# Lp pooling on one core: the first load goes out as two halves of 64 rows, on two queues

## The chip, the core and the metric

The kernel runs on one core of a Trainium2 chip. The metric is the device time of one launch in microseconds, the median of several runs; lower is better. The core's engines take part as follows: ScalarE (ACT) squares and takes roots, VectorE (DVE) adds, SyncE (SP) and ScalarE issue the transfers between HBM and SBUF, and 16 DMA engines carry them out. TensorE and GpSimd compute nothing here.

## The reference

```python
x: float32 [32, 256, 4096]; p = 2.0; kernel_size = 4
out_length = length // kernel_size            # 1024
for i in range(out_length):
    window = np.abs(x[:, :, 4 * i:4 * i + 4]) ** p
    result[:, :, i] = np.mean(window, axis=-1) ** (1.0 / p)
```

With p = 2 this is, for every four neighbours, the square root of the mean of their squares. 134.2 MB are read and 33.6 MB are written.

## The kernel before

The input is taken as one flat array, since windows of four never cross a channel. It is cut into six blocks (`blocks`, line 51), each block into 128 rows, one for each SBUF partition, and the rows of a block into tiles along their length. There are 20 tiles; most are 128 x 13184 floats (`W`, 52,736 bytes in each partition, 6592 KB in all), the last is 128 x 11680. Three tiles fit at a time: tile i lies in `x_tiles[i % 3]`, printed `xt` in the profile.

Each tile goes through the same steps:

- `load(i)` (line 79, its DMA on line 83) brings the tile in with one DMA on SP's queue.
- `square` (line 89, ACT) squares it in place.
- `pairs` (line 95, DVE) adds elements 0 and 2, and 1 and 3, of each window, into the first half of the same tile.
- `fours` (line 99, DVE) adds the two sums of each window into the output tile `ot`, into the PSUM tile `st` or into a free part of an `xt`.
- `root` (line 102, ACT) takes the square root of a quarter of the sum, for one to three tiles at a time.
- `store(b, queue)` (line 86) writes a block of four tiles back with one DMA: blocks 0 to 2 are issued on the ACT queue, blocks 3 to 5 on SP.

The order of instructions on each engine is written out by hand (`manual_schedule`), and the framework adds the semaphore waits that the data need. Where one wait already follows from another, `implied(later, earlier)` (line 118) takes it away:

```python
    def implied(later, earlier):

        tc.declare_no_dep(later.ins, earlier.ins, reason="implied by the other waits")

    for i in range(X_SLOTS):
        load(i)
```

Loads 0, 1 and 2 are issued at once, ahead of everything else. In the loop over tiles 0 to 16 (line 130), load i + 3 stands behind the two sums of tile i: SP waits for them, as the slot is free only then. ACT's first instructions are the load of its function table and a root of one column (`first`), and then the square of tile 0, which waits for load 0.

Block 4 is stored by `store(4, nc.sync)` and block 5, the last tile alone, by `store(5, nc.sync)`, which is the last transfer of the program.

Of the kernel before, what the change touches and what calls it, by code (L numbers as in the profile page):

```python
# [1 line left out]

# [4 lines left out]


@with_exitstack
def kernel(  # L10
    ctx: ExitStack,
    tc: tile.TileContext,
    x: bass.AP,
    p: float,
    kernel_size: int,
    out: bass.AP,
):

    nc = tc.nc

    assert float(p) == 2.0, "kernel specialized for p == 2"
    k = int(kernel_size)  # L30
    assert k == 4, "kernel specialized for kernel_size == 4"

    P = nc.NUM_PARTITIONS
    fp32 = mybir.dt.float32
    Act = mybir.ActivationFunctionType
    add = mybir.AluOpType.add
    xf = x.rearrange("b c l -> (b c l)")
    of = out.rearrange("b c l -> (b c l)")
    total = xf.shape[0] // P

    W = 13184
    R = W // k
    X_SLOTS = 3
    NARROW = W - 32
    LAST = total - 18 * W - NARROW
    widths = [W] * 3 + [NARROW] + [W] * 15 + [LAST]
    n = len(widths)
    assert 0 < LAST <= W and LAST % 16 == 0


    blocks = [[0, 1, 2, 3], [4, 5, 6, 7], [8, 9, 10, 11], [12, 13, 14, 15], [18, 16, 17], [19]]
    block_of = {i: b for b, group in enumerate(blocks) for i in group}
    block_width = [sum(widths[i] for i in group) for group in blocks]

    x_pool = ctx.enter_context(tc.tile_pool(name="x_pool", bufs=1))
    o_pool = ctx.enter_context(tc.tile_pool(name="o_pool", bufs=1))
    s_pool = ctx.enter_context(tc.tile_pool(name="s_pool", bufs=1, space=bass.MemoryType.PSUM))
    x_tiles = [x_pool.tile([P, W], fp32, name=f"xt{j}") for j in range(X_SLOTS)]
    o_tile = o_pool.tile([P, 4 * R], fp32, name="ot")
    first = o_pool.tile([P, 1], fp32, name="first")  # L60
    s_tile = s_pool.tile([P, 4096], fp32, name="st")
    ctx.enter_context(tc.manual_schedule())

    def rows(flat, b, div):
        at = sum(block_width[:b]) * P // div
        return flat[at:at + block_width[b] * P // div].rearrange("(p w) -> p w", p=P)


    free = x_tiles[17 % X_SLOTS]
    place = {i: o_tile[:, i % 4 * R:i % 4 * R + widths[i] // k] for i in range(16)}  # L70
    place[18] = free[:, R:2 * R]
    place[19] = free[:, 0:LAST // k]
    place[16] = free[:, 2 * R:3 * R]
    place[17] = free[:, 3 * R:4 * R]
    held = [o_tile[:, 0:w // k] for w in block_width[:4]] + [free[:, R:4 * R], place[19]]

    xs, loads, stores, sums, squares = {}, {}, {}, {}, {}

    def load(i):
        b = block_of[i]  # L80
        at = sum(widths[j] for j in blocks[b][:blocks[b].index(i)])
        xs[i] = x_tiles[i % X_SLOTS][:, 0:widths[i]]
        loads[i] = nc.sync.dma_start(out=xs[i], in_=rows(xf, b, 1)[:, at:at + widths[i]])  # L83

    def store(b, queue):
        stores[b] = queue.dma_start(out=rows(of, b, k), in_=held[b])  # L86

    def square(v):
        return nc.scalar.activation(out=v, in_=v, func=Act.Square)  # L89

    def pairs(v):

        q = v.rearrange("p (n j) -> p n j", j=k)
        h = v[:, 0:v.shape[1] // 2].rearrange("p (n j) -> p n j", j=2)
        return nc.vector.tensor_tensor(out=h, in0=q[:, :, 0:2], in1=q[:, :, 2:4], op=add)  # L95

    def fours(o, v):
        h = v[:, 0:v.shape[1] // 2].rearrange("p (n j) -> p n j", j=2)
        return nc.vector.tensor_tensor(out=o, in0=h[:, :, 0], in1=h[:, :, 1], op=add)  # L99

    def root(o, s):
        return nc.scalar.activation(out=o, in_=s, func=Act.Sqrt, scale=1.0 / k)  # L102

    summed = {i: s_tile[:, 0:R] if i in (4, 8, 12, 16) else place[i] for i in range(n)}

    def roots(*group):
        if len(group) == 1:
            root(place[group[0]], summed[group[0]])
        else:
            v = o_tile[:, group[0] % 4 * R:(group[-1] % 4 + 1) * R]  # L110
            r = root(v, v)
            if group[0] in (5, 9):

                implied(r, stores[block_of[group[0]] - 1])
        if group[-1] in (3, 7, 11):
            store(block_of[group[-1]], nc.scalar)
# [9 lines that stand above are left out]
    ahead = {4: (3,), 8: (7,), 12: (11,)}  # L126
    behind = {3: [(0, 1, 2)], 7: [(5, 6), (4,)], 11: [(9, 10), (8,)], 14: [(12,)], 15: [(13, 14)], 16: [(15,)]}

    root(first[:, :], nc.const_aps.tensor(1.0, (P, 1), fp32))
    for i in range(17):  # L130
        if i in ahead:
            roots(*ahead[i])
        s = square(xs[i])
        squares[i] = s
        if i == 3:
            implied(s, squares[0])
        if i in (3, 7, 11):

            for earlier in sums[i - X_SLOTS]:
                implied(s, earlier)  # L140
        for group in behind.get(i, []):
            roots(*group)
        sums[i] = pairs(xs[i]), fours(summed[i], xs[i])
        if i + X_SLOTS < n:
            load(i + X_SLOTS)

    store(3, nc.sync)
    square(xs[17])
    pairs(xs[17])
    fours(summed[17], xs[17])  # L150
    later = {18: 4608, 19: 2000}

    def shared_square(i):
        v = xs[i][:, 0:later[i]]
        nc.vector.tensor_tensor(out=v, in0=v, in1=v, op=mybir.AluOpType.mult)  # L155
        square(xs[i][:, later[i]:widths[i]])

    def shared_pairs(i):
        implied(pairs(xs[i]), loads[i])

    shared_square(18)
    roots(16)
    roots(17)
    shared_pairs(18)
    fours(summed[18], xs[18])
    shared_square(19)
    roots(18)
    store(4, nc.sync)
    shared_pairs(19)
    fours(summed[19], xs[19])  # L170
    roots(19)
    store(5, nc.sync)


# [1 line left out]
_INS = ['x', 'p', 'kernel_size']  # L176
_OUTS = [((32, 256, 1024), 'float32')]

_NUMBERS = {'p': 2.0, 'kernel_size': 4}


# [26 lines left out]
```

## Time and profile before

| What | us |
|---|---|
| Median of 3 runs (394.01 to 394.08) | 394.02 |
| The profiled execution's own time | 394.04 |
| Span of its profile | 392.3 |
| ACT busy | 274.4 (70%) |
| DVE busy | 218.2 (56%) |
| Packets of the SP queue (q1), share of 16 DMA engines | 87.4% |
| Packets of the ACT queue (q10), share of 16 DMA engines | 11.9% |
| Mean rate over the span | 428 GB/s |

The profiled execution's time stands 1.7 us above its span; that part lies outside the recorded instructions. Times in the views count from the start of the span. The DMA queue lines give packets, megabytes and the time that the packets took, as a share of what 16 DMA engines could have worked in the span. In the chain of waits, each piece is what held up the next one, followed back from the last instruction. In the windows view, the DMA share is 1.00 where all 16 engines are busy; a packet's bytes count at its start, so that in short windows the rate swings and only its place in time is to be read.

### The profile page before, as it was taken

What the parts mean: (1) busy time and instruction counts of PE and PEld (TensorE: products, weight loads), DVE (VectorE), ACT (ScalarE), POOL (GpSimd) and SP (SyncE); (2) the same over time, 40 slices, a digit from 0 to 9 for tenths busy, and PEclk for the clock granted to TensorE, in tenths of its full rate; (3) what the DMA queues carried; (4) which work ended last, traced back from release to release, by engine and by line L of the source; (5) the groups of instructions that cost most, each with busy time, mean ns of one, the idle gap of its engine ahead of it and who ended that gap; (6) DMA issues with size and microseconds to landing.
All of it is one profiled execution on the core that took longest, in us unless ns stands there. A gap on an engine that the chain in (4) does not pass through costs nothing.

```text
span 392.3 us, 176 instructions
## 1 busy us (share of the span) xinstructions
DVE 218.2 (56%) x42; ACT 274.4 (70%) x37; POOL 0.2 (0%) x4
## 2 busy tenths in 40 slices
DVE  0009477580693274905942748069418485699970
ACT  1095695979950859799509597995098999969910
POOL 0000000000000000000000000000000000000000
DMA  8999999999999999999999999999999999999997
GB/s 344 430 430 430 430 440 435 452 457 366 430 430 430 430 430 430 430 441 446 452 446 441 436 430 436 430 430 430 430 430 430 430 430 430 430 453 415 430 413 342
DMA packets 3744, 167.77 MB, mean 428 GB/s; under 512 B 416, under 2 KB 416, under 8 KB 416
## 3 DMA queue, kind: packets, MB, share of 16 engines
q1 hardware_dynamic: 3312, 147.53, 87.4%
q10 hardware_dynamic: 432, 20.25, 11.9%
HBM read 134.22 MB, written 33.55 MB: 428 GB/s over the span
## 4 chain that ended last, share of the span: by engine, by line
DMA 43%; ACT 30%; DVE 23%; issue 0%; ACTq 0%; SPq 0%; DVEq 0%
DMA xt<-in_x_dram 43%; ACT xt L89 28%; DVE xt L95 14%; DVE ot L99 5%; DVE xt L99 3%; DVE xt L155 2%; ACT ot L102 2%; ACT xt L102 1%; ACTq L86 0%; SPq L83 0%; DVEq L95 0%
## 5 line engine op out<-in xcount | busy, mean ns | idle before, releaser
L89 ACT ACTIVATE xt<-xt 128x13184 f32<-128x13184 f32 (+3 forms) x20 | 216.7, 10847 | 92.3 <-DMA xt<-in_x_dram 91.0
L95 DVE TENSOR_TENSOR xt<-xt 128x6592 f32<-128x6592 f32 (+2 forms) x20 | 139.7, 6985 | 144.1 <-ACT xt L89 143.9
L99 DVE TENSOR_TENSOR ot<-xt 128x3296 f32<-128x3296 f32 (+1 forms) x13 | 46.7, 3592 | 17.9 <-DMA out_dram<-ot 17.6
L102 ACT ACTIVATE ot<-ot 128x6592 f32<-128x6592 f32 (+3 forms) x8 | 37.2, 4655 | 7.0 <-DVE ot L99 7.0
L102 ACT ACTIVATE xt<-xt 128x3296 f32<-128x3296 f32 (+1 forms) x3 | 8.5, 2836 | 8.8 <-DVE xt L99 8.8
L99 DVE TENSOR_TENSOR st<-xt 128x3296 f32<-128x3296 f32 x4 | 14.4, 3600 | 0.1
L99 DVE TENSOR_TENSOR xt<-xt 128x3296 f32<-128x3296 f32 (+1 forms) x3 | 10.4, 3461 | 0.1
L102 ACT ACTIVATE ot<-st 128x3296 f32<-128x3296 f32 x3 | 8.7, 2898 | 0.0
L155 DVE TENSOR_TENSOR xt<-xt 128x4608 f32<-128x4608 f32 (+1 forms) x2 | 7.2, 3593 | 0.0
L102 ACT ACTIVATE xt<-st 128x3296 f32<-128x3296 f32 x1 | 2.9, 2898 | 0.0
L102 ACT ACT_TABLE_LOAD x1 | 1.3, 1283 | 0.7 <-PEq L189 0.7
L102 ACT ACTIVATE first<-const-float32-1.0 128x1 f32<-128x1 f32 x1 | 0.2, 202 | 0.0
L189 POOL MEMSET const-bfloat16-1.0<- 128x1 bf16 x1 | 0.1, 101 | 0.0
L189 POOL MEMSET const-uint8-127<- 128x1 uint8 x1 | 0.1, 101 | 0.0
L189 POOL MEMSET const-float32-0.0<- 128x1 f32 x1 | 0.1, 98 | 0.2 <-issue 0.2
L189 POOL MEMSET const-float32-1.0<- 128x1 f32 x1 | 0.1, 98 | 0.0
## 6 DMA issues: line engine op xcount, KB each, us to landing
xt<-in_x_dram SPq DMA_DIRECT2D x18, 6592.0 KB, 29.8
out_dram<-ot ACTq DMA_DIRECT2D x2, 6592.0 KB, 35.1
out_dram<-ot SPq DMA_DIRECT2D x1, 6592.0 KB, 37.1
out_dram<-ot ACTq DMA_DIRECT2D x1, 6588.0 KB, 36.3
xt<-in_x_dram SPq DMA_DIRECT2D x1, 6576.0 KB, 24.7
xt<-in_x_dram SPq DMA_DIRECT2D x1, 5840.0 KB, 21.9
out_dram<-xt SPq DMA_DIRECT2D x1, 4944.0 KB, 16.1
out_dram<-xt SPq DMA_DIRECT2D x1, 1460.0 KB, 8.2
```

Source lines behind the costliest of these rows:

```text
L89: return nc.scalar.activation(out=v, in_=v, func=Act.Square)
L95: return nc.vector.tensor_tensor(out=h, in0=q[:, :, 0:2], in1=q[:, :, 2:4], op=add)
L99: return nc.vector.tensor_tensor(out=o, in0=h[:, :, 0], in1=h[:, :, 1], op=add)
L102: return nc.scalar.activation(out=o, in_=s, func=Act.Sqrt, scale=1.0 / k)
L155: nc.vector.tensor_tensor(out=v, in0=v, in1=v, op=mybir.AluOpType.mult)
L189: nc = _bacc.Bacc("TRN2", target_bir_lowering=False, num_devices=1)
```

## The change

Load 0 becomes two DMAs of 64 rows each. Rows 64 to 127 go out on the ScalarE queue, as ACT's first instruction, ahead of its table load; rows 0 to 63 go out on SP, in load 0's old place. All other loads stay as they were. Since load 0 is now two transfers, load 3 (the next one into the same slot) and the two sums of tile 0 would wait for both; these waits are declared away, because the sums wait for the square, which waits for both halves, and load 3 waits for the sums.

```diff
+    halves = []
 
     def load(i):
         b = block_of[i]
         at = sum(widths[j] for j in blocks[b][:blocks[b].index(i)])
         xs[i] = x_tiles[i % X_SLOTS][:, 0:widths[i]]
-        loads[i] = nc.sync.dma_start(out=xs[i], in_=rows(xf, b, 1)[:, at:at + widths[i]])
+        v = rows(xf, b, 1)[:, at:at + widths[i]]
+        if i == 0:
+            halves.append(nc.scalar.dma_start(out=xs[i][P // 2:P, :], in_=v[P // 2:P, :]))
+            halves.append(nc.sync.dma_start(out=xs[i][0:P // 2, :], in_=v[0:P // 2, :]))
+        else:
+            loads[i] = nc.sync.dma_start(out=xs[i], in_=v)
+            if i == X_SLOTS:
+                for half in halves:
+                    implied(loads[i], half)
...
         sums[i] = pairs(xs[i]), fours(summed[i], xs[i])
+        if i == 0:
+            for half in halves:
+                for s in sums[i]:
+                    implied(s, half)
         if i + X_SLOTS < n:
             load(i + X_SLOTS)
```

## The prediction, on record before the changed kernel ran

> **What bounds the kernel now.** I read the page's DMA queues first, then the chain of waits, then the windows, and last the first five microseconds.
>
> From the page:
>
> ```profile
> span 392.3 us, 176 instructions
> ...
> DMA  8999999999999999999999999999999999999997
> ...
> q1 hardware_dynamic: 3312, 147.53, 87.4%
> q10 hardware_dynamic: 432, 20.25, 11.9%
> ```
>
> The two queues' packets fill 87.4 + 11.9 = 99.3% of what 16 DMA engines can do in the span, 389.5 of 392.3 us. Only the first and the last slice are not full. The kernel is bound by its transfers from the first row to the last, and there is no idle DMA time in the middle into which a late start could vanish. ACT (70%) and DVE (56%) have room.
>
> The chain of waits and the timeline (start, duration, what; in the timeline, what ended the idle time before it):
>
> ```profile
> 0.73 18.04 DMA xt<-in_x_dram
> ...
> 18.79 11.20 ACT xt L89
> ...
> 30.01 7.04 DVE xt L95
> ...
> 37.07 3.60 DVE ot L99
> ...
> 40.75 24.70 DMA xt<-in_x_dram
> ```
>
> ```profile
> 0.73 1.28 ACT L102 ACT_TABLE_LOAD   x1 [0.73 <-PEq L189]
> ...
> 18.79 11.19 ACT L89 ACTIVATE xt<-xt 128x13184 f32<-128x13184 f32 x1 [16.56 <-DMA xt<-in_x_dram]
> ...
> 34.35 11.19 ACT L89 ACTIVATE xt<-xt 128x13184 f32<-128x13184 f32 x1 [4.38 <-DMA xt<-in_x_dram]
> ...
> 49.94 11.19 ACT L89 ACTIVATE xt<-xt 128x13184 f32<-128x13184 f32 x1 [4.39 <-DMA xt<-in_x_dram]
> ```
>
> The chain names load 0, then the work on tile 0, then load 3. That is a chain by waits; what paces it is the queue. Loads 0, 1 and 2 land 15.56 and 15.59 us apart (the three squares start on the landings). Load 3 is issued at 40.75, when load 2 still has until 49.94 to run: 9.2 us of cover. A whole load is 128 rows on 16 DMA engines, 8 rows for each, so a row takes 15.56 / 8 = 1.945 us.
>
> The windows (start:end, length, DVE, ACT and POOL busy, clock, DMA share, GB/s), and the queues between 94 and 110 us, where a store on the ACT queue runs beside a load on SP:
>
> ```profile
> 40.00:84.00 44.00, 29.19 (x7) 35.26 (x4) 0.00 (x0) 1.00 0.97 422
> 94.00:110.00 16.00, 8.01 (x2) 16.00 (x2) 0.00 (x0) 1.00 0.97 422
> 130.00:165.00 35.00, 20.26 (x5) 29.63 (x4) 0.00 (x0) 1.00 1.00 434
> ```
>
> ```profile
> q10 hardware_dynamic: 72, 3.79, 54.7%
> q1 hardware_dynamic: 72, 2.95, 42.7%
> ```
>
> Loads alone and a load beside a store run at the same 422 GB/s. With two queues at work each got 72 packets in that stretch: they take turns, one for one.
>
> The start (same columns; bytes count at a packet's start):
>
> ```profile
> 1.60:1.80 0.20, 0.00 (x0) 0.20 (x1) 0.00 (x0) 1.00 5.24 1582
> 1.80:2.00 0.20, 0.00 (x0) 0.20 (x1) 0.00 (x0) 1.00 4.30 1318
> 2.40:2.60 0.20, 0.00 (x0) 0.00 (x0) 0.00 (x0) 1.00 0.63 264
> 2.80:4.20 1.40, 0.00 (x0) 0.00 (x0) 0.00 (x0) 1.00 0.00 0
> 4.20:4.40 0.20, 0.00 (x0) 0.00 (x0) 0.00 (x0) 1.00 1.22 527
> 4.60:4.80 0.20, 0.00 (x0) 0.00 (x0) 0.00 (x0) 1.00 5.48 2373
> ```
>
> SP issues load 0 at 0.73, its 16 first rows begin between 1.6 and 2.6, and the second rows between 4.2 and 5.0.
>
> **The change, part by part.**
>
> The issue. SP still issues three loads at the start (the group of three took 1.33 us), the first with half the rows. ACT issues one DMA more, ahead of its table load: 0.34 to 0.38 us by the three stores that it issues later (line 86). The table load (1.28 us) and the one-column root (0.20) move behind it. All of it lies inside the 16.56 us in which ACT waits for tile 0, and costs nothing; without that cover it would cost the 0.38. That ACT really issues first is not in doubt: nothing stands ahead of it, and its queue is let go at 0.73, as SP's is.
>
> The waits. The square of tile 0 now waits for two landings, not one. The waits of tile 0's sums and of load 3 on the halves are declared away, so they stay as they were. In the built program the framework puts waits on the halves back further down, at the pairs of tile 3 on DVE and at load 6 on SP; both are long met there. Where DVE now waits for two things at once (tiles 18 and 19) the chain shows 0.02 + 0.04 = 0.06 us of it. At tile 3, DVE has been idle 4.86 us for ACT, and load 6 has 9 us of queued transfers ahead of it: nothing. Each landing has a semaphore lane that rotates by one place for all later transfers; the transfers that shared a lane are still tens of microseconds apart.
>
> The transfer itself is the term that decides. The trace has no DMA of fewer than 128 rows; all 26 transfers spread over all 128 partitions. So the two halves are bounded from both sides by whole loads. Low end: each half takes half of a load's 15.56 us, the two share the engines, and tile 0 lands when it did: 0. An earlier start may give a little: two queues that hand out the first rows together could halve the 1.0 us over which these begin, so -0.5 at most. High end: a half takes as long as a whole load, since the rate of about 430 GB/s belongs to the 128 partitions as much as to the 16 engines, and 64 partitions offer half of it. Then tile 0 takes 2 x 15.56 us, which is +15.56.
>
> That both halves are in flight together would not rescue the high end. They are issued at the same 0.73, and two queues take turns row for row, so that all 16 engines would work on rows of the lower half, then all on the upper half, and so on. If 64 partitions offer half the paths, two of the 16 rows in flight always meet on one path into the tile, and each row takes 2 x 1.945 us. Two rows that meet share only while both run: if one engine is d ahead of the other, 8 rows lose 8 x (1.945 - d). The second rows begin over some 0.8 us, but it is the closest of the pairs that sets the landing; I take d = 0.1, which gives 8 x 1.845 = 14.8, and keep 12.4 (d = 0.4) to 15.6 (d = 0).
>
> I take the high end. The rows cannot decide, for a limit of the engines and one of the partitions would give the same 422 GB/s in every stage shown. What tips it is that the kernel is at its transfer limit throughout: a transfer of a new shape can gain 0.5 us there and lose 15.6. [...]
>
> Pass-through. Tile 0 lands at 18.8 + 14.8 = 33.6, and its sums, and so load 3, come as much later; but loads 1 and 2 stand behind the halves and move too, so the 9.2 us of cover in front of load 3 stays. With 99.3% of the DMA time full, nothing takes the delay back, up to the last store. The sum: 394.04 + 14.8 = 408.8, set against the profiled execution's own 394.04; the median, 394.02, is the same within 0.02.
>
> **Rivals.**
>
> 1. Not slower: the engines alone are the limit, and 64 rows run as fast for each row as 128. For it speaks that a load beside a store makes 422 GB/s, as loads alone do, so that a second direction adds nothing to the total. Against it, that this fits a limit on the way into the tile as well. It decides if the first square starts by about 18.8. Then the time is 394.04 less 0 to 0.5: 393.9. Should ACT's half come late, load 1's rows fill the gap, tile 0 lands later by as much, and the 9.2 us of cover take it. Faster by over 0.2% (0.8 us, about what a measurement of this kernel can tell from no change) would need more than the whole 0.5 that the spread of the first rows offers.
>
> 2. The rows meet, but fall out of step: where of two rows on one path one goes first and the other waits, the first engine is a row ahead and the two work on different halves from then on. That costs one row, 1.95 us: 396.0. If it takes several rows, 1.95 for each: 398 to 405. For it speaks that the first rows don't start together (1.6 to 2.6); against it, that queues and engines in the trace take turns evenly, and fair sharing keeps the distance d as it is.
>
> **How the numbers follow.** The halves at half the rate: 0.58, at 408.8, its own range 405 to 411 (two rows may cost a little more than double). Out of step after one to five rows: 0.14. Not slower: 0.28, of which 0.22 lie within 0.2% and 0.06 for a gain above 0.8 us by something at the start that the trace doesn't show. Slower: 0.58 + 0.14 = 0.72. To leave out no more than 2 in 10, the range must take in the 0.28 as well: 393.4 to 411.
>
> **What would show it.** Right: the first square starts at 32 to 35, not 18.8; the second 15.6 later, as before; the window from 4 to 30 shows about 220 GB/s with packets of twice the time, and q1's share of the engines grows by some 4%. After that every line is the old one, moved by the same amount. Wrong: a first square at about 18.5 with 422 GB/s from the start (rival 1), or at 20.7 to 30 with a slow stretch of a few us (rival 2). The forecast also fails if the first square is late but the last store is not: then there was room in the transfers that the 99.3% hide.

## The result and the profile after

The changed kernel takes 409.85 us (median, 409.69 to 410.02) against 394.01 for the kernel before, measured with it. The ratio is 1.0402, 95% interval 1.0388 to 1.0415. The profiled execution took 409.75, with a span of 407.7.

From the page of the changed kernel, the span, the DMA share, the rate by slice and the queues:

```profile
span 407.7 us, 180 instructions
...
DMA  9998999999999999999999999999999999999997
GB/s 202 212 248 331 414 414 444 465 414 414 435 471 419 414 424 476 424 414 414 476 435 414 414 461 450 414 414 440 471 414 414 424 481 419 414 459 407 466 393 333
...
q1 hardware_dynamic: 3248, 144.15, 83.8%
q10 hardware_dynamic: 512, 23.62, 15.4%
```

The DMA engines are as busy as before, 83.8 + 15.4 = 99.2%. But in the first three slices, some 30 us, they move half as much. A share of busy time cannot show that; the rate beside it does.

The chain of waits and the timeline of the changed kernel:

```profile
0.72 36.53 DMA xt<-in_x_dram
```

```profile
0.72 0.54 SPq L87 DMA_DIRECT2D xt<-in_x_dram  x1
0.72 0.55 ACTq L86 DMA_DIRECT2D xt<-in_x_dram  x1
1.30 1.28 ACT L111 ACT_TABLE_LOAD   x1 [1.30 <-PEq L202]
...
37.27 11.19 ACT L98 ACTIVATE xt<-xt 128x13184 f32<-128x13184 f32 x1 [34.47 <-DMA xt<-in_x_dram]
...
50.92 11.19 ACT L98 ACTIVATE xt<-xt 128x13184 f32<-128x13184 f32 x1 [2.45 <-DMA xt<-in_x_dram]
...
66.50 11.19 ACT L98 ACTIVATE xt<-xt 128x13184 f32<-128x13184 f32 x1 [4.39 <-DMA xt<-in_x_dram]
```

Both halves are issued at 0.72. Tile 0 lands 18.5 us later than before, tiles 1 and 2 both 16.56 later (50.92 against 34.35, 66.50 against 49.94).

Windows of the changed kernel, and the queues between 4 and 30 us:

```profile
4.00:16.00 12.00, 0.00 (x0) 0.00 (x0) 0.00 (x0) 1.00 1.00 211
16.00:30.00 14.00, 0.00 (x0) 0.00 (x0) 0.00 (x0) 1.00 1.03 218
56.00:100.00 44.00, 31.17 (x6) 35.28 (x4) 0.00 (x0) 1.00 0.99 426
```

```profile
q10 hardware_dynamic: 58, 3.06, 55.3%
q1 hardware_dynamic: 58, 2.53, 46.1%
```

At 211 GB/s an engine moves 13.2, and a row of 52,736 bytes takes 4.0 us, where it took 1.945. Each queue has 58 packets between 4 and 30 us; ten of SP's are under 512 bytes, so 48 of its rows stand beside 58 of ACT's. Behind the halves the rate is the old one.

The two queues share the engines in whole turns. The packets that begin between 1 and 9 us, between 9 and 13, and between 13 and 17:

```profile
q1 hardware_dynamic: 32, 1.69, 99.4%
...
q10 hardware_dynamic: 16, 0.84, 98.5%
...
q1 hardware_dynamic: 16, 0.84, 98.1%
```

SP's first 32 rows go ahead of any of ACT's; from then on 16 rows of one half and 16 rows of the other take turns. So in each turn all 16 engines work on the same half of the tile, as the prediction had assumed, and a row takes 3.9 us (0.985 x 4.0).

### The profile page after: what moved, and what is told of

The parts are those of the page before. It is cut to its first block, busy times and chain, and to the rows that moved or that the text cites. A ratio compares the mean times of both kernels' runs of the same rounds, so it can differ in the third digit from the quotient of the medians.

```text
span 407.7 us, 180 instructions
## 1 busy us (share of the span) xinstructions
DVE 218.2 (54%) x42; ACT 274.4 (67%) x37; POOL 0.2 (0%) x4
## 3 DMA queue, kind: packets, MB, share of 16 engines
q1 hardware_dynamic: 3248, 144.15, 83.8%
q10 hardware_dynamic: 512, 23.62, 15.4%
## 4 chain that ended last, share of the span: by engine, by line
DMA 46%; ACT 29%; DVE 22%; issue 0%; ACTq 0%; SPq 0%; DVEq 0%
DMA xt<-in_x_dram 46%; ACT xt L98 27%; DVE xt L104 14%; DVE ot L108 4%; DVE xt L108 3%; DVE xt L168 2%; ACT ot L111 1%; ACT xt L111 1%; ACTq L95 0%; SPq L89 0%; DVEq L104 0%
```

## The experiments

Row times below come from windows: GB/s times the window's length is the bytes of the packets that began in it, so many rows; the DMA share times the length times 16 is the engine time that these rows took.

**Is it the rows or the queues?** Both halves on one queue:

```diff
-            halves.append(nc.scalar.dma_start(out=xs[i][P // 2:P, :], in_=v[P // 2:P, :]))
+            halves.append(nc.sync.dma_start(out=xs[i][P // 2:P, :], in_=v[P // 2:P, :]))
```

> Both halves go out on SP, one behind the other; ACT issues nothing at the start. Theory A (64 neighbouring partitions offer half of the paths into the tile): rows take 3.93 us as in the change, the first square starts at 34 to 37, and loads 1 and 2 land some 16 us late. The time is 410 to 411: as the change, and about 1 us more if the first use of the ACT queue costs 1 us at 91 us again. Theory B (two queues at work on one tile, or on HBM, hinder each other): rows take 1.95 us, the time is 394.0 to 394.3.

Measured: 410.81 us, ratio 1.0422 (1.0408 to 1.0436). The windows of this kernel:

```profile
4.00:33.00 29.00, 0.00 (x0) 0.00 (x0) 0.00 (x0) 1.00 0.99 204
34.00:54.00 20.00, 6.53 (x1) 13.58 (x2) 0.00 (x0) 1.00 1.01 422
```

The second queue is not needed for the loss: 204 GB/s with one, 215 with two (the changed kernel between 4 and 30), or 4.1 us a row against 3.9. The time is 1 us more than the changed kernel's, as expected, but not for the reason given: no slow rows came back at the first store (16 rows that begin between 109 and 110 us take 1.95 us each). Loads 1 and 2 land 17.26 later than in the kernel before, not 16.56.

Two queues, but cut by columns instead of rows:

```diff
-            halves.append(nc.scalar.dma_start(out=xs[i][P // 2:P, :], in_=v[P // 2:P, :]))
-            halves.append(nc.sync.dma_start(out=xs[i][0:P // 2, :], in_=v[0:P // 2, :]))
+            H = widths[i] // 2
+            halves.append(nc.scalar.dma_start(out=xs[i][:, H:], in_=v[:, H:]))
+            halves.append(nc.sync.dma_start(out=xs[i][:, 0:H], in_=v[:, 0:H]))
```

> Two queues as in the change, but load 0 is cut by columns: each half has all 128 rows and 6592 columns (26,368 bytes for each row). Theory A: every row keeps its own path, rows take half of 1.95 us, 0.97, and tile 0 lands at about 18.8 to 20; the time is 393.0 to 394.0, 393.2 if the first use of the ACT queue at the start takes the place of the 1 us that it costs at 91 us. Theory B: the first load takes twice as long, 409 to 410.

Measured: 394.37 us, ratio 1.0007 (0.9999 to 1.0016), a little above the 393.0 to 394.0 expected of theory A and far from theory B's 409. Between 4 and 16 us the two queues make 422 GB/s; the first square starts at 19.21, 0.4 us later than in the kernel before. Here two queues at work on one tile lose nothing that the time can tell, and starting with two queues gains nothing.

**Which rows?** Load 0 in a middle part and two outer ones:

```diff
-            halves.append(nc.scalar.dma_start(out=xs[i][P // 2:P, :], in_=v[P // 2:P, :]))
-            halves.append(nc.sync.dma_start(out=xs[i][0:P // 2, :], in_=v[0:P // 2, :]))
+            halves.append(nc.scalar.dma_start(out=xs[i][32:96, :], in_=v[32:96, :]))
+            halves.append(nc.sync.dma_start(out=xs[i][0:32, :], in_=v[0:32, :]))
+            halves.append(nc.sync.dma_start(out=xs[i][96:P, :], in_=v[96:P, :]))
```

> Load 0 in three: rows 32 to 95 on the ACT queue, rows 0 to 31 and then 96 to 127 on SP. Each of the 16 DMA engines has 4 rows of the middle part and 2 of each outer part. [...] Theory C (a transfer of 64 or fewer rows is slow whichever rows they are): 409 to 411. Theory B: 409 to 410.

Measured: 403.11 us, ratio 1.0228 (1.0214 to 1.0242). The windows of this kernel:

```profile
5.00:8.00 3.00, 0.00 (x0) 0.00 (x0) 0.00 (x0) 1.00 1.37 281
12.40:13.20 0.80, 0.00 (x0) 0.00 (x0) 0.00 (x0) 1.00 2.46 1055
14.40:15.30 0.90, 0.00 (x0) 0.00 (x0) 0.00 (x0) 1.00 4.29 938
```

Each of these windows holds the start of 16 rows, one for each engine (281 x 3.0, 1055 x 0.8 and 938 x 0.9 are all 843 to 844 KB). They took 1.37 x 3.0 = 4.1 us, 2.46 x 0.8 = 1.97 us and 4.29 x 0.9 = 3.9 us. The queues of the same three windows tell whose rows they are:

```profile
q1 hardware_dynamic: 16, 0.84, 137.5%
...
q10 hardware_dynamic: 16, 0.84, 245.1%
...
q1 hardware_dynamic: 16, 0.84, 429.5%
```

So slow and full-speed rows stand beside each other in one load. The full-speed ones are ACT's, rows 32 to 95, a transfer of 64 rows, which refutes theory C; the rows of 3.9 and 4.1 us are SP's, the outer part. Only one of the four turns of middle rows ran wholly at full speed. In the other three slow rows were still under way, and 16 rows took 2.7, 2.4 and 2.4 us each (between 9.4 and 12.4 us a share of 0.91 over 3.0 us; between 18 and 20, and 24 and 26, 1.22 and 1.21 over 2.0). That is 1.7 us in all, which is why the time lies above the 400 to 402 that middle rows at full speed and outer ones at half would make (an estimate from the row times: 4 x 1.95 + 4 x 3.9 = 23.4 us for an engine, 7.8 more than the 15.6 of a whole load, less the 1 us that the kernel before loses at store 0, told below).

The runs show which groups of rows are slow and which are not; which partitions share a path into the tile they do not show.

**Is it HBM's side?** The same halves of the tile, filled from every second row of the block:

```diff
+            w = v.rearrange("(q two) w -> two q w", two=2)
-            halves.append(nc.scalar.dma_start(out=xs[i][P // 2:P, :], in_=v[P // 2:P, :]))
-            halves.append(nc.sync.dma_start(out=xs[i][0:P // 2, :], in_=v[0:P // 2, :]))
+            halves.append(nc.scalar.dma_start(out=xs[i][P // 2:P, :], in_=w[1]))
+            halves.append(nc.sync.dma_start(out=xs[i][0:P // 2, :], in_=w[0]))
```

> The change with other rows of HBM: partitions 0 to 63 get rows 0, 2, 4 ... 126 of the block and partitions 64 to 127 get rows 1, 3 ... 127, so that tile 0's results lie in other rows than the reference's. Theory A (the destination partitions are what half of the paths belong to): nothing changes, rows take 3.93 us, 409.6 to 410.1. Rival D (the 64 rows of a half lie together in HBM, and that is what slows them): rows take 1.95 us, 393.5 to 395.

Measured: 409.97 us, ratio 1.0401 (1.0387 to 1.0414), with 211 GB/s between 4 and 16 us. Which rows of HBM fill a half made no difference here (409.85 us with rows that lie together); with the middle rows above, this leaves the destination partitions.

**Does it grow with the length of the rows?** A part of load 0's columns as two 64-row transfers, the rest whole, all on SP, once with T = 512 and once with T = 4096:

```diff
-            halves.append(nc.scalar.dma_start(out=xs[i][P // 2:P, :], in_=v[P // 2:P, :]))
-            halves.append(nc.sync.dma_start(out=xs[i][0:P // 2, :], in_=v[0:P // 2, :]))
+            T = 512
+            for r in (slice(0, P // 2), slice(P // 2, P)):
+                halves.append(nc.sync.dma_start(out=xs[i][r, 0:T], in_=v[r, 0:T]))
+            halves.append(nc.sync.dma_start(out=xs[i][:, T:], in_=v[:, T:]))
```

> Load 0 in three, all on SP: 512 columns as two transfers of 64 rows, then the other 12672 columns as one of 128 rows. Theory A charges only the thin part twice: 512 / 13184 of 15.56 us, 0.6 us more at tile 0, plus up to 0.5 us for two more transfers. It also asks what the change's slow start gave back at load 5 (1.2 us): if any stretch of rows that share a path is enough for it, the rows at 92 us take 1.95 us and the time is 393.4 to 394.0; if it takes a long one, they stay slow, and the time is 394.6 to 395.2.

> As the run with 512 columns, with 4096: two transfers of 64 rows of 16,384 bytes on SP, then the other 9088 columns as one of 128 rows. The 512 columns took about 84 ns a row where 76 is the full rate, so that short rows showed little of a shared path. Theory A for long rows: 16,384 bytes take 1.2 us, not 0.6, and tile 0 lands 4096 / 13184 of 15.56 us later, 4.8, or 4 to 5.5 with the start. The time is 398 to 399.5 if the rows at 92 us then run at 1.95 us (the change's 1.2 us given back), 399 to 400.5 if not. If rows of 16 KB take 0.6 us, 394.5 to 395.5, the sharing would need longer rows than these.

Measured: 395.50 us (ratio 1.0039, 1.0027 to 1.0051) and 398.67 us (1.0117, 1.0100 to 1.0134). With T = 4096, between 4 and 6 us:

```profile
4.00:6.00 2.00, 0.00 (x0) 0.00 (x0) 0.00 (x0) 1.00 1.15 238
```

476 KB are 29 rows of 16,384 bytes, and 1.15 x 2.0 x 16 = 36.8 us make 1.27 us a row; at full rate it is 0.6. So the loss follows the bytes that go in halves. With T = 512 the time is 0.3 above the expected 394.6 to 395.2, and the first square starts 1.4 us late; most of it is that the large part is now the third transfer on SP and is issued at 1.96, not 0.73. That leaves some 0.2 us for the thin part (1.4 less 1.23), where theory A charged 0.6; its rows of 2,048 bytes do not show the sharing, and the run says little on theory A.

**Do the declared-away waits matter?** The change without them:

```diff
-            if i == X_SLOTS:
-                for half in halves:
-                    implied(loads[i], half)
...
-        if i == 0:
-            for half in halves:
-                for s in sums[i]:
-                    implied(s, half)
```

> The change without the declared-away waits: the pairs of tile 0 on DVE and load 3 on SP wait for both halves as well, the pairs of tile 3 no longer do. All of these landings are long met. If the declarations are worth nothing: 409.8 to 410.0, every landing as in the change within 0.1 us. If each extra wait on the path costs 0.06 us, the shift of tile 0's pairs, it stays hidden behind the queue all the same. More than 0.4 us in either direction would make them a part of the result.

Measured: 409.84 us, ratio 1.0398 (1.0385 to 1.0412). They are worth nothing that can be measured.

**What was given back, 1.2 us.** The changed kernel is 16.56 us late at tiles 1 and 2, but only 15.31 at tile 6 (its square starts at 144.17 against 128.86), and stays there. In between lies store 0. Windows of the kernel before, and of the changed one, just ahead of its rows:

```profile
92.00:93.00 1.00, 0.00 (x0) 1.00 (x1) 0.00 (x0) 1.00 2.51 738
```

```profile
108.00:109.00 1.00, 0.00 (x0) 1.00 (x1) 0.00 (x0) 1.00 1.95 844
```

In the kernel before 14 rows took 2.51 x 16 / 14 = 2.87 us each, 0.9 more than a row should; in the changed one 16 rows took 1.95. The kernel before loses about 1 us there, and the changed one does not; the rest of the 1.2 is not accounted for. If that loss could be avoided by itself, there would be a kernel faster than both, so four runs looked for its cause, each with one edit to the kernel before. First, a small transfer so that store 0 is no longer the first on the ACT queue:

```diff
+    tiny = o_pool.tile([16, 128], fp32, name="tiny")
+    nc.scalar.dma_start(out=tiny[:, :], in_=xf[0:2048].rearrange("(p w) -> p w", p=16))
```

> The kernel before, with one DMA of 16 rows of 512 bytes into a tile of its own as the first instruction on the ACT queue; load 0 is whole, on SP. It takes the first use of the ACT queue from the store at 90 us to the start. Theory F (the first DMA on a queue holds up the rows in flight by about 1 us, all engines): the 16 rows at 92 us take 1.95 us, not 2.6 to 3.1, the start is 0 to 0.4 us later, and the time is 393.0 to 393.5. Rival (the slow rows at 92 us come from the store's own start, whichever DMA was first on its queue): they stay at 2.6 to 3.1 us, and the time is 394.0 to 394.4.

Then store 0 on the other queue:

```diff
-            store(block_of[group[-1]], nc.scalar)
+            store(block_of[group[-1]], nc.sync if group[-1] == 3 else nc.scalar)
```

> The kernel before with store 0 alone moved from the ACT queue to SP, where it stands behind load 6. It asks where the 1 us of slow rows at 92 us comes from. Theory G (it comes from the second queue joining a full first one): no rows above 2.1 us but the first ones, 392.9 to 393.4. Theory H (it comes with the first write to HBM, whichever queue): the slow rows move to about 112 us, 394.0 to 394.3.

Store 0 a little later:

```diff
+            if group[-1] == 3:
+                for _ in range(5):
+                    root(first[:, :], nc.const_aps.tensor(1.0, (P, 1), fp32))
             store(block_of[group[-1]], nc.scalar)
```

> The kernel before with five one-column roots ahead of store 0 on ACT, so that the store is issued about 1 us later, half a row, and all else as before. If the slow rows at 92 us depend on where in a row the store's descriptors arrive: no slow rows, 392.9 to 393.4. If not: they move by 1 to 2 us, and the time stays at 394.0 to 394.3.

And a small store at the start, so that store 0 is not the first write:

```diff
+    nc.gpsimd.memset(tiny[:, :], 0.0)
+    nc.scalar.dma_start(out=of[0:2048].rearrange("(p w) -> p w", p=16), in_=tiny[:, :])
```

> The kernel before with a store of 16 rows of 512 bytes at the start, on the ACT queue, from a small tile that GpSimd sets to zero; store 0 later writes over the same place. It asks whether the 1 us of slow rows ahead of store 0 is paid once, by the first write to HBM of the launch. If so, it moves to the start, beside the slow first rows, and the rows at 92 us take 1.95 us: 392.9 to 393.5. If it belongs to store 0 itself: slow rows at 92 us as before, 394.0 to 394.4.

Measured, in this order: 394.23 us (ratio 1.0004, 0.9995 to 1.0013), 394.74 (1.0024, 1.0005 to 1.0043), 394.30 (1.0005, 0.9996 to 1.0013) and 394.16 (1.0002, 0.9993 to 1.0011). None is faster. With the small transfer first, the load's rows between 91.5 and 93.7 us, and between 93.7 and 95.2:

```profile
q1 hardware_dynamic: 16, 0.84, 94.2%
...
q1 hardware_dynamic: 12, 0.63, 147.7%
```

The first are 2.07 us a row (0.942 x 2.2), nearly the full speed that theory F asked for, but slow rows still come, one row later: 1.477 x 1.5 x 16 / 12 = 2.95 us. In this run store 0 is issued at 90.60, in the kernel before at 90.31. One window of each of the other three, in the same order:

```profile
108.00:110.00 2.00, 1.97 (x2) 2.00 (x1) 0.00 (x0) 1.00 1.10 343
```

```profile
94.00:95.00 1.00, 0.00 (x0) 1.00 (x1) 0.00 (x0) 1.00 2.57 738
```

```profile
92.00:93.00 1.00, 0.00 (x0) 1.00 (x1) 0.00 (x0) 1.00 2.56 791
```

Rows of 2.7 us (13 rows in 1.10 x 2 x 16), 2.9 us (14 rows) and 2.7 us (15 rows): the slow rows follow store 0 to about 108 us on the SP queue, and come 2 us later when it is issued later (91.22). The first use of the queue, the first write of the launch and the point within a row are not their cause. Where load 0 was cut by columns, and so began on both queues, they are there too (between 92 and 93 us 13 rows of 2.6 us: a share of 2.15, 686 GB/s). They are missing in the changed kernel and with both halves on one queue (1.95 us a row in both, as above), with the middle rows (11 rows between 101 and 102 us take 1.95: a share of 1.34, 580 GB/s) and with T = 4096, where ten rows begin between 97 and 98 us and take 1.95 us, while with T = 512 they are there (2.9 us). Why they are missing after a slow start stays open. The window with store 0 on SP is of an execution of 399.06 us.

## Why the prediction was right, and where it was off

**The bound: right. The pass-through: right but for 1.2 us.** The prediction said that nothing takes the delay back. What the first load lost did come out at the end, since nothing in the transfers was idle, except for the 1.2 us at store 0, most of which came of rows in the kernel before that were slow though their engines counted as busy. The last load's square starts 15.37 us later (376.00 against 360.63); the span is 15.4 longer, and another 0.3 lies outside the span (409.75 - 407.7 against 394.04 - 392.3).

**The high end for a 64-row transfer: right, and now shown.** It was taken on an argument of what can be gained and lost, with no row to decide it. That argument says what is at stake and not which end is true, so by the rows the choice was a guess, and a chance of 0.28 and the lower end of the range were kept for the other. The queues by turn, the middle rows, the columns and the HBM rows decide it: where all engines worked on rows 0 to 63 of the tile, or all on rows 64 to 127, a row took 3.9 to 4.1 us, and 1.945 in a whole load.

**The distance d: the term that was mis-sized.** The forecast took 0.1 us off each of 8 rows for engines that are not quite in step, 14.8 in all. Loads 1 and 2 are 16.56 late. Some 0.3 of that is a later start: in the changed kernel no row begins before 2.0 us, in the kernel before they begin from 1.6 to 1.8 on. The rest, 16.26, is 2.03 for each of 8 rows, slightly more than 1.945, where I had put 1.845. Three windows of the changed kernel show how it comes about, each with the start of 16 rows:

```profile
5.00:9.00 4.00, 0.00 (x0) 0.00 (x0) 0.00 (x0) 1.00 1.03 211
9.00:13.00 4.00, 0.00 (x0) 0.00 (x0) 0.00 (x0) 1.00 0.98 211
33.00:35.00 2.00, 0.00 (x0) 0.00 (x0) 0.00 (x0) 1.00 1.19 422
```

Where the queues alternate a row takes 3.9 us, where two turns of one half follow each other 4.1, and load 1's first rows, which begin while ACT's last are still under way, take 2.4 instead of 1.95. Being out of step saved nothing. Whether the rows that share a path were in step, or the sharing is not as I had it, the trace doesn't say, since it doesn't name the paths. The own range, 405 to 411, held it because it allowed for more than double. I had counted the start as free or a gain; both issues took 0.54 and 0.55 us, where one took 0.38, and ACT's rows did not begin together with SP's.

**Tile 0's landing: 37.25, forecast 33.6.** The first square, at 37.27, is outside the 32 to 35 that was to show the forecast right. Besides the above, tile 1 follows tile 0 after 13.65 us instead of 15.56. The difference, 1.9 us, is about one row: a row of load 1 went ahead of the last completion of ACT's half. Between 30.5 and 34.6 us 16 rows begin, all of load 1 on SP; between 34.6 and 37 come the 16 small packets that end ACT's half, beside the next 16 rows:

```profile
q1 hardware_dynamic: 16, 0.84, 81.2%
q10 hardware_dynamic: 16, 0.00, 0.4%
```

The transfers lose nothing by it, but load 3 is issued at 59.24 with 7.3 us of cover left, not 9.2 as I had it. It was still enough.

**The small terms: right.** ACT's extra issue and the later table load stay inside its wait for tile 0, now 34.47 us. The waits cost nothing with or without the declarations. One sign was wrong: q1's share was to grow by some 4%, and it fell from 87.4% to 83.8%. It is the ACT queue's share that grew, from 11.9% to 15.4%, since half of load 0 now goes there.

**The rivals.** The engines alone are not the limit (rival 1): they count as busy at 211 GB/s as at 422. Nor do the rows fall out of step (rival 2): 218 GB/s between 16 and 30 us is half the rate still, and the turns stay whole. The forecast of 408.8 was 1.05 below 409.85: rows 1.8 us longer in all than I had them (16.56 - 14.8, the start included), 1.2 given back at store 0, and 0.3 outside the span, with 0.1 of rounding and scatter. That it came so close is partly luck: without the 1.2, which no term foresaw, it would have been more than 2 us too low.

## What to carry to other kernels

Where a kernel is bound by its transfers, look at the rate and not only at the busy share: here the engines counted as 99% busy while they moved half as much. A load cut at partition 64 ran at half the rate, whether its halves went on one queue or two (204 and 215 GB/s against 422), and with rows of 16,384 bytes (1.27 us a row against 0.6) as with rows of 52,736 (3.9 to 4.1 against 1.945); one cut by columns did not (422 GB/s), nor did rows 32 to 95 where no slow rows were under way beside them (1.97 us a row). Before a start is reworked, ask what it could give at most (here an estimated 0.5 us) and what the new shape of the transfer could cost.

## What the runs showed of the hardware that was not expected

- A transfer of 64 rows can run at full speed: 1.97 us a row for the middle part in the turn that it had to itself, against 3.9 to 4.1 for the outer ones.
- The rows just ahead of the first full store took 2.6 to 2.95 us, in the kernel before and wherever load 0 had no long stretch of slow rows, whether that store was on the ACT queue or on SP. In the changed kernel, with both halves on one queue, with the middle rows and with T = 4096, all of which began with such a stretch, they took 1.95. The cause was not found.
- With two queues, the completion of one can stand behind a whole row of the other: 1.9 us here, on the landing of tile 0.
- Two queues that are issued to at the same time do not have to begin together: here the first 32 rows were all SP's, and the column cut began with 16 of SP's.
